# A block with 32 experts on one core: the order of ScalarE's and VectorE's work among the experts, the PSUM banks, and how far weights are split ahead

## The chip, the cores and the metric

The kernel runs on one core of a Trainium2 chip. The metric is the device time of one execution in microseconds. Before the change it is 2903.58 us, the median of three runs (2898.73 to 2910.64).

## The reference, cut to what matters

A first block of two hybrid layers (a linear recurrence beside attention, then a feed-forward network), then a second block with an mLSTM mixer and a mixture of experts, all in float32 for 512 tokens of 1024 channels. The change touches only the experts:

```python
logits = (xt @ w_router + b_router)                  # 512 tokens, 32 experts
top_vals, top_idx = lax.top_k(logits, TOP_K)         # TOP_K = 4
top_gates = jax.nn.softmax(top_vals, axis=-1)
...
def expert_block(args):                              # xb: tokens of one expert
    xb, e = args
    gate = xb @ w_gate[e] + b_gate[e]                # 1024 x 1024
    up = xb @ w_up[e] + b_up[e]                      # 1024 x 1024
    gate = jnp.minimum(gate, SWIGLU_LIMIT)
    up = jnp.clip(up, -SWIGLU_LIMIT, SWIGLU_LIMIT)
    glu = gate * jax.nn.sigmoid(SWIGLU_ALPHA * gate)
    return (glu * (up + 1.0)) @ w_down[e] + b_down[e]
...
y_buf = y_buf * gate_buf[:, None]
out = jax.ops.segment_sum(y_buf, tok_buf, num_segments=T + 1)[:T]
```

Each expert has 12 MB of weights, which are read once: 384 loads of 1 MB.

## The kernel before

**Experts by rank.** `rank` (L1331) sorts the experts by their number of tokens. `ranked` (L1823) runs through them in a fixed order of ranks, `FEW`, that mixes large and small ones. Rank 31 comes first; then, with t for a twin, 1 for one block of 128 tokens and 2 for two blocks: t 2 t t 1 t 2 t t 1 t t 2 t t 1 t t 2 t t 1 t t 2 t t 1 t 1 t. So there are 20 twins, 7 experts of one block (with rank 31) and 5 of two blocks: two of (128, 128) and three of (128, 64).

**A split expert** (one or two blocks) has float32 weights that TensorE multiplies in parts: a tile `w` with the part `hi`, rounded by a ScalarE copy, and the rest `lo`, made by a VectorE subtraction from `raw` (`split`, L244 and L245). A product is then three matmuls (`lin`: x high by hi, x high by lo, x low by hi), or two for a block of 64, whose high and low rows share one operand. **A twin** (`twin`, up to 64 tokens) uses the loaded tile `raw` itself: gate fills one half of TensorE's columns and up the other, and nothing is split.

**Stages of an expert.** gate and up are computed in two halves n = 0, 1 of 512 of the 1024 inner channels (`gate_up`, L1630; `gate_up_twin`, L1657). A half has eight steps, k = 0 to 7, one for each 128 input channels, and each step uses one half-tile of 1024 columns, so a 1 MB load serves two steps. `gated` (L1678) then makes the activations: a Silu on ScalarE (L1693, for twins L1674) and two VectorE operations (L1691 and L1694, for twins L1675 and L1676), four more for a block of 64. `turn` (L1696) transposes them on TensorE and copies them out of PSUM. `down` (L1716) and `down_twin` (L1733) multiply them with eight half-tiles, then the result is scaled on ScalarE (`scaled`, L1766; L1747 for twins) and added into the output by an indirect DMA (`scatter`, L1753). `block` and `find` (L1498, L1512) make the one-hot rows of the next expert's tokens, search their numbers and gate weights with small matmuls and gather their rows; `fetch` (L1536) transposes those rows.

**The loop** interleaves two experts: gate/up half 0 of the current one (with the search for the next one and, after some 4 us, the transposition of the previous one's second activations among its steps), then down of the previous one, then gate/up half 1 of the current one (with the transposition of its first activations at step 0, and after some 4 us the `fetch` of the next one). `tiles` turns a time into a step: 0.9 us a step for a twin, 1.4 for a block of 128, 0.95 more for a block of 64.

**What sets the order.** `with self.tc.manual_schedule(engines={mybir.EngineType.PE})` keeps TensorE's instructions in the order in which the program issues them. The other engines' instructions are put in an order by a planner when the program is built; it goes by its own estimate of when each could start. On the chip each engine then runs its queue in that order, and an instruction that waits holds up those behind it.

**Weights** come out of `weights` (L1607), one half-tile a call:

```python
self.split_ahead(AHEAD + 1)                     # AHEAD = 3
self.catch_up(CU + len(self.later) // CV)       # pending operations, CU = 1, CV = 6
return self.halves.pop(0)
```

`split_ahead` (L1585) issues loads into a ring of nine 1 MB tiles and splits into a ring of four `w`. It goes on until four split halves or twelve halves in all are ready, and the whole halves of twins don't count among the four. `catch_up` (L1612) issues operations of `later`, the list of what follows the last sums: the parts of `gated` and `scaled`.

**PSUM.** The eight banks: four for gate and up (tag `gu`), two for down (`dn`), two for transposes and searches (`tps`). A (128, 128) expert takes four `gu` banks for each half, a twin one.

Of the kernel before, what the change touches and what calls it, by code (L numbers as in the profile page):

```python
# [6 lines left out]
F32 = mybir.dt.float32  # L7
# [10 lines left out]
P = 128  # L18
# [187 lines left out]
class _Kernel:  # L206
# [1124 lines left out]
    def rank(self, tp):  # L1331

        nc, cst, rp, mo = self.nc, self.cst, self.rp, self.mo
        hold = lambda shape, name, dt=F32: rp.tile(shape, dt, name=name)
        keep = lambda shape, name, dt=F32: tp.tile(shape, dt, name=name)
        bank = lambda: self.ps2.tile([P, T], F32, tag="gu", name="gu", bufs=4)
        e32, p32 = cst[:, C_E32:C_E32 + NE], cst[:, C_P32:C_P32 + 1]
        t0 = bank()
        for j in range(4):
            nc.tensor.transpose(t0[0:NE, j * P:(j + 1) * P], self.pos[:, j], self.ident)  # L1340
        pT = mo.tile([P, T], F32R, tag="g", name="pT", bufs=2)[0:NE]
        nc.scalar.activation(pT, t0[0:NE], AF.Copy)
        t1 = bank()
        for j in range(4):
            nc.tensor.transpose(t1[0:96, j * P:(j + 1) * P], self.G[:, j].rearrange("p a e -> p (a e)"), self.ident)
        self.gT = gT = mo.tile([P, T], F32R, tag="g", name="gT", bufs=2)[0:96]
        kc = keep([96, 1], "kc")
        nc.vector.scalar_tensor_tensor(kc, self.cc, 32.0, cst[0:96, C_KEYC:C_KEYC + 1], op0=OP.mult, op1=OP.subtract)
        cmp_ = keep([96, NE], "cmp")
        nc.vector.tensor_scalar(cmp_, self.krow[0:96], kc, None, op0=OP.is_gt)  # L1350
        rk = keep([96, 1], "rk")
        nc.vector.reduce_sum(rk, cmp_, axis=AX.X)
        self.perm = hold([96, NE], "perm", F32R)
        nc.vector.tensor_scalar(self.perm, e32[0:96], rk, None, op0=OP.is_equal)
        pb = keep([NE, NE], "permb", BF16)
        nc.vector.tensor_copy(pb, self.perm[0:NE].bitcast(F32))
        t2 = bank()
        self.mm(t2[0:1, 0:NE], self.p32b[0:NE], pb, True, True)
        self.order = hold([1, NE], "order", I32)
        nc.vector.tensor_copy(self.order, t2[0:1, 0:NE])  # L1360
        self.orderf = hold([1, NE], "orderf")
        nc.vector.tensor_copy(self.orderf, t2[0:1, 0:NE])
        self.split_rows(gT, t1[0:96])
        t3 = bank()
        for j in range(4):
            self.mm(t3[:, NE * j:NE * j + NE], pT[:, j * P:(j + 1) * P], self.perm[0:NE], j == 0, j == 3)
        self.posS = hold([P, 4, NE], "posS")
        nc.vector.tensor_copy(self.posS, t3[:, 0:4 * NE].rearrange("p (j e) -> p j e", j=4))
        self.posB = hold([P, 4, NE], "posB")
        nc.vector.tensor_scalar(self.posB, self.posS, -128.0, None, op0=OP.add)  # L1370
        t4 = bank()
        for j in range(4):
            self.mm(t4[:, NE * j:NE * j + NE], gT[0:64, j * P:(j + 1) * P], self.perm[0:64], j == 0, j == 3)
        self.gates = hold([P, 4, NE, 6], "gates", BF16)
        nc.gpsimd.tensor_copy(self.gates[..., 3:6], self.tok[:, :, None, :].to_broadcast([P, 4, NE, 3]))
        self.parts(self.gates[..., 0:3], t4[:, 0:4 * NE].rearrange("p (j e) -> p j e", j=4),
                   mo.tile([P, 4, NE], F32, tag="bs", name="gr", bufs=4))

        cnt = mo.tile([NE, P], F32R, tag="bs", name="cnt", bufs=4)
        nc.gpsimd.tensor_copy(cnt, self.cc[0:NE].to_broadcast([NE, P]))  # L1380
        t5 = bank()
        self.mm(t5[:, 0:NE], cnt, self.perm[0:NE], True, True)
        self.count = hold([P, NE], "count")
        nc.vector.tensor_copy(self.count, t5[:, 0:NE])

        over = keep([1, NE], "over")
        nc.vector.tensor_tensor(over, self.count[0:1], cst[0:1, C_FEW:C_FEW + NE], op=OP.is_gt)
        most = keep([1, 1], "most")
        nc.vector.reduce_max(most, over, axis=AX.X)
        self.many = hold([1, 1], "many", I32)  # L1390
        nc.vector.tensor_copy(self.many, most)
# [13 lines left out]
    def down_bias(self, j):  # L1405

        nc = self.nc
        y = self.mo.tile([P, D], F32, tag="yy", name="yb", bufs=3)
        for n in range(2):
            p, w = self.ps2.tile([P, T], F32, tag="dn", name="dn", bufs=2), slice(n * T, (n + 1) * T)  # L1410
            self.mm(p, self.gT[:, j * P:(j + 1) * P], self.bd[:, w], True, True)
            nc.scalar.activation(y[:, w], p, AF.Copy)
        nc.gpsimd.dma_start(self.acc_d[j * P:(j + 1) * P, :], y, accum_op=OP.add)
# [170 lines left out]

    def split_ahead(self, n):  # L1585


        nc = self.nc
        while self.todo and len(self.halves) < 2 * NRAW - 6:
            src, i, whole = self.todo[0]  # L1590
            if not whole and sum(lo is not None for _, lo in self.halves) >= n:
                break
            self.todo.pop(0)
            if i == 0:
                self.raw = self.raws[self.nload % NRAW]
                self.nload += 1
                nc.sync.dma_start(self.raw, src)
            raw = self.raw[:, 1024 * i:1024 * i + 1024]
            if whole:
                self.halves.append((raw, None))  # L1600
                continue
            w = self.ws[self.nsplit % (AHEAD + 1)]
            self.nsplit += 1
            self.split(raw, w[:, 0], w[:, 1])
            self.halves.append((w[:, 0], w[:, 1]))

    def weights(self):  # L1607
        self.split_ahead(AHEAD + 1)
        self.catch_up(CU + len(self.later) // CV)
        return self.halves.pop(0)  # L1610

    def catch_up(self, n=None):  # L1612
# [17 lines left out]
    def gate_up(self, n, bsel, blocks, among=()):  # L1630

        nc, mo = self.nc, self.mo
        among = list(among)
        if blocks[0]["twin"]:
            return self.gate_up_twin(n, bsel, blocks[0], among)
        ps = [[self.ps2.tile([P, T], F32, tag="gu", name="gu", bufs=4) for _ in range(2)] for _ in blocks]
        for c in range(4):
            for i in range(2):
                wt = self.weights()
                k = 2 * c + i  # L1640
                for p, b in zip(ps, blocks):
                    for s in range(2):
                        w = slice(s * T, (s + 1) * T)
                        self.product(p[s], b, b["xt"], k, [x if x is None else x[:, w] for x in wt], k == 0, k == KD - 1)
                        if k == 0:
                            o = s * D + n * T
                            self.mm(p[s][0:b["n"]], bsel[:, 0:b["n"]], self.bias[:, o:o + T], False, False)
                self.step(among, k)
        for p, b in zip(ps, blocks):
            b["u%d" % n] = self.slot()[0:b["n"]]  # L1650
            self.later += self.gated(p, b["n"], b["u%d" % n])
# [5 lines left out]
    def gate_up_twin(self, n, bsel, b, among):  # L1657


        p = self.ps2.tile([P, T], F32, tag="gu", name="gu", bufs=4)  # L1660
        for k in range(KD):
            w, _ = self.weights()
            for s in range(2):
# [51 lines left out]

    def down(self, n, blocks):  # L1716
        nc, mo = self.nc, self.mo
        ps = [self.ps2.tile([P, T], F32, tag="dn", name="dn", bufs=2) for _ in blocks]
        for c in range(2):
            for i in range(2):  # L1720
                wt = self.weights()
                for z in range(2):
                    k, w = 2 * i + z, slice(z * T, (z + 1) * T)
                    for p, b in zip(ps, blocks):
                        self.product(p, b, b["h%d" % c], k, [x[:, w] for x in wt], c == 0 and k == 0, c == 1 and k == 3)
        for p, b in zip(ps, blocks):
            if n == 0:
                b["y"] = mo.tile([P, D], F32, tag="yy", name="yy", bufs=3)
            self.later += self.scaled(p, b, n)
        if len(blocks) > 1:  # L1730
            self.catch_up()

    def down_twin(self, b):  # L1733

        nc = self.nc
        p = self.ps2.tile([P, T], F32, tag="dn", name="dn", bufs=2)
        rows = (p[0:64], p[64:P])
        for c in range(2):
            w = [self.weights()[0] for _ in range(4)]
# [83 lines left out]
    def ranked(self, cur, slots, ranks, more=False):  # L1823
# [28 lines left out]
            k = tiles(cur, us)  # L1852
            return [(k + i, f) for i, f in enumerate([f for b in nxt for f in self.fetch(b)])]

        with self.tc.manual_schedule(engines={mybir.EngineType.PE}):
            nxt = start(ranks[0], blocks_of(ranks[0]))
            self.queue(order[1][0])
            self.gate_up(1, *cur, [(0, lambda: self.turn(cur[1], 0))])
# [51 lines left out]

SILU7 = 11.914 / (1.0 + _np.exp(-11.914))
ASIDE = (3, 1)
NRAW = 9
RAW0 = 5
XG = 2
EARLY = 2
CU = 1
# [62 lines left out]
```

## Time and profile before

| | |
|---|---|
| median of three runs | 2903.58 us |
| profiled execution, its span | 2903.9 us, 2902.0 us |
| TensorE (PE) busy | 2728.3 us, 94% |
| VectorE (DVE), ScalarE (ACT) busy | 1583.9 us, 55%; 1124.0 us, 39% |
| mean granted clock of TensorE | 0.972 |
| read from HBM | 607.31 MB |

The first 55% of the span are the first block and the mixer; the experts run from some 1690 us to the last sums at 2875 us. In the views below a line names an engine, a line of the kernel, an operation, and `out<-in` by the program's names. The page's slices are each 1/40 of the span, 72.6 us, and their digits busy shares in tenths. A row of waits gives engine and line, what it waited for, the total in us, how often, and the longest. A row of windows gives a stretch, its length, the busy us of each engine with its instructions, the granted clock of TensorE as a share of 2.4 GHz, the DMA share and GB/s; the sum row adds the stretches of one question. A row of the timeline gives start and length in us, and in brackets the idle time of the engine before it and what ended that. A row of groups gives count, busy us, mean ns, then idle us before them and what ended it.

### The profile page before, as it was taken

What the parts mean: (1) busy time and instruction counts of PE and PEld (TensorE: products, weight loads), DVE (VectorE), ACT (ScalarE), POOL (GpSimd) and SP (SyncE); (2) the same over time, 40 slices, a digit from 0 to 9 for tenths busy, and PEclk for the clock granted to TensorE, in tenths of its full rate; (3) what the DMA queues carried; (4) which work ended last, traced back from release to release, by engine and by line L of the source; (5) the groups of instructions that cost most, each with busy time, mean ns of one, the idle gap of its engine ahead of it and who ended that gap; (6) DMA issues with size and microseconds to landing.
All of it is one profiled execution on the core that took longest, in us unless ns stands there. A gap on an engine that the chain in (4) does not pass through costs nothing. (4 is left out here: it accounts for less than half of the span.)

```text
span 2902.0 us, 33795 instructions
## 1 busy us (share of the span) xinstructions
PE 2728.3 (94%) x12644; PEld 1927.0 (66%) x12644; DVE 1583.9 (55%) x2601; ACT 1124.0 (39%) x1655; POOL 217.6 (7%) x207
## 2 busy tenths in 40 slices
PE   7989999999999999999999889989999999999985
PEld 5677888888877788888777656546446446446452
DVE  7877676365686663333488664354444345335353
ACT  3644442222554442222344344344333334334342
POOL 0100000000000000000011010110100210110100
PEclk8999999999999999999999989999999999999998
DMA  6332446365221233333221586997997998998995
GB/s 230 122 113 93 160 160 223 118 213 165 94 69 59 65 99 102 95 96 99 89 73 62 190 317 266 338 409 295 384 399 304 346 407 354 366 409 320 371 386 214
DMA packets 126078, 629.42 MB, mean 217 GB/s; under 512 B 15632, under 2 KB 19088, under 8 KB 76752
## 3 DMA queue, kind: packets, MB, share of 16 engines
q1 hardware_dynamic: 111744, 593.94, 54.2%
q0 software_dynamic: 8288, 23.86, 3.8%
q10 hardware_dynamic: 5872, 9.36, 0.9%
q8 instruction: 101, 1.65, 0.2%
q14 instruction: 73, 0.60, 0.1%
HBM read 607.31 MB, written 24.38 MB: 218 GB/s over the span
## 5 line engine op out<-in xcount | busy, mean ns | idle before, releaser
L236 PE MATMUL acc<-hh,whi 128*128 128x512 f32 (+1 forms) x1496 | 574.7, 388 | 13.9 <-ACT hh L506 6.2
L236 PE MATMUL acc<-hh,wlo 128*128 128x512 f32 (+1 forms) x1496 | 576.5, 387 | 5.2 <-DVE wlo L245 5.1
L236 PE MATMUL acc<-hl,whi 128*128 128x512 f32 (+1 forms) x1496 | 574.2, 385 | 0.7 <-DVE hl L507 0.7
L245 DVE TENSOR_TENSOR wlo<-raw,whi 128x1024 fp32r<-128x1024 f32 (+2 forms) x253 | 305.6, 1210 | 268.4 <-ACT whi L244 266.7
L245 DVE TENSOR_TENSOR w<-raw,w 128x1024 fp32r<-128x1024 f32 x288 | 341.1, 1219 | 188.7 <-ACT w L244 186.9
L244 ACT ACTIVATE whi<-raw 128x1024 fp32r<-128x1024 f32 (+2 forms) x253 | 258.9, 1024 | 471.5 <-PE acc L236 417.9
L236 PE MATMUL gu<-w,xth 128*128 128x512 f32 x896 | 313.9, 429 | 44.1 <-ACT w L244 29.0
L244 ACT ACTIVATE w<-raw 128x1024 fp32r<-128x1024 f32 x288 | 293.0, 1051 | 111.6 <-PE gu L236 67.5
L236 PEld LDWEIGHTS acc<-hh,whi 128*128 128x128 f32 x1496 | 282.1, 190 | 78.5 <-ACT hh L506 9.0
L236 PEld LDWEIGHTS acc<-hh,wlo 128*128 128x128 f32 x1496 | 283.3, 189 | 62.4 <-DVE wlo L245 6.3
L236 PEld LDWEIGHTS acc<-hl,whi 128*128 128x128 f32 x1496 | 283.6, 190 | 56.4 <-issue 3.1
L236 PE MATMUL gu<-raw,xf 128*64 128x512 f32 x1280 | 305.8, 601 | 0.7 <-ACT xf L1549 0.7
L236 PEld LDWEIGHTS gu<-w,xth 128*128 128x128 f32 x896 | 173.3, 198 | 100.4 <-ACT w L244 42.7
L236 PE MATMUL gu<-w,xtl 128*128 128x512 f32 x448 | 183.4, 409 | 0.0
L236 PEld LDWEIGHTS gu<-raw,xf 128*64 128x64 f32 x1280 | 82.3, 136 | 128.8 <-issue 122.7
L236 PE MATMUL dn<-w,hTh 128*128 128x512 f32 x448 | 148.0, 407 | 20.5 <-ACT w L244 11.5
L236 PE MATMUL dn<-raw,hf 128*64 128x512 f32 x640 | 143.0, 600 | 0.0
L236 PEld LDWEIGHTS dn<-w,hTh 128*128 128x128 f32 x448 | 85.2, 192 | 56.3 <-ACT w L244 17.6
L1675 DVE TENSOR_SCALAR u<-gu 64x512 f32<-64x512 f32 x40 | 27.3, 682 | 159.7 <-ACT g L1674 159.7
L828 DVE TENSOR_TENSOR t<-t,acc 128x512 f32<-128x512 f32 x44 | 30.3, 688 | 143.6 <-PE acc L236 134.6
L236 PEld LDWEIGHTS dn<-raw,hf 128*64 128x64 f32 x640 | 45.3, 138 | 89.8 <-issue 89.7
L1753 POOL DMA_INDIRECT accd<-yy,idx x37 | 58.3, 1576 | 590.8 <-ACT yy L1766 264.3
(685 smaller groups left out, 3914.8 us busy)
## 6 DMA issues: line engine op xcount, KB each, us to landing
raw<-in_wgu SPq DMA_DIRECT2D x256, 1024.0 KB, 12.5
raw<-in_wd SPq DMA_DIRECT2D x128, 1024.0 KB, 12.3
raw<-in_ws SPq DMA_DIRECT2D x220, 512.0 KB, 3.5
adaw<-in_wada SPq DMA_DIRECT2D x72, 512.0 KB, 4.8
raw<-in_wada SPq DMA_DIRECT2D x24, 512.0 KB, 5.0
raw<-in_ws SPq DMA_DIRECT2D x24, 384.0 KB, 3.0
xy<-in_xT SPq DMA_DIRECT2D x16, 256.0 KB, 4.6
raw<-in_ws SPq DMA_DIRECT2D x9, 256.0 KB
```

The costliest lines, as they stand in the source:

```text
L236: self.nc.tensor.matmul(ps, l, r, start=first, stop=last)
L244: self.nc.scalar.activation(hi, src, AF.Copy)
L245: self.nc.vector.tensor_sub(lo, src, hi.bitcast(F32))
L828: nc.vector.tensor_mul(u, s, ps[1])
L1675: lambda: nc.vector.tensor_scalar(u, p[0:64], 8.0, -6.0, op0=OP.min, op1=OP.max),
L1753: self.nc.gpsimd.indirect_dma_start(out=self.acc_d[:, :], out_offset=bass.IndirectOffsetOnAxis(ap=b["idx"][0:m, 0:1], axis=0), in_=b["y"][ ...
```

## The change

ScalarE (Activation) and VectorE (DVE) are kept in program order among the experts, as TensorE is. gate, up and down take their sums from one tag of six banks. `split_ahead` counts whole halves too, so that three halves, of whatever kind, are ahead of the one that is handed out. `weights` issues pending operations first and then the next split.

```diff
-        bank = lambda: self.ps2.tile([P, T], F32, tag="gu", name="gu", bufs=4)
+        bank = lambda: self.ps2.tile([P, T], F32, tag="gu", name="gu", bufs=6)
...
-            p, w = self.ps2.tile([P, T], F32, tag="dn", name="dn", bufs=2), slice(n * T, (n + 1) * T)
+            p, w = self.ps2.tile([P, T], F32, tag="gu", name="dn", bufs=6), slice(n * T, (n + 1) * T)
...
     def split_ahead(self, n):
-        while self.todo and len(self.halves) < 2 * NRAW - 6:
-            src, i, whole = self.todo[0]
-            if not whole and sum(lo is not None for _, lo in self.halves) >= n:
-                break
-            self.todo.pop(0)
+        while self.todo and len(self.halves) < n:
+            src, i, whole = self.todo.pop(0)
...
     def weights(self):
+        self.catch_up(CU + len(self.later) // CV)
         self.split_ahead(AHEAD + 1)
-        self.catch_up(CU + len(self.later) // CV)
         return self.halves.pop(0)
...
-        with self.tc.manual_schedule(engines={mybir.EngineType.PE}):
+        with self.tc.manual_schedule(engines=IN_ORDER):
...
+IN_ORDER = {mybir.EngineType.PE, mybir.EngineType.Activation, mybir.EngineType.DVE}
```

The tags `gu` in `gate_up` and `gate_up_twin` and `dn` in `down` and `down_twin` change in the same way.

## Rows read from the trace of the kernel before

**Rows 1.** The page: mean busy share of the DMA engines in 40 slices.

```profile
DMA  6332446365221233333221586997997998998995
```

**Rows 2.** Waits of PE, 1640 to 2902 us.

```profile
PE gu L236 <- ACT w L244: 29.0, 17, 1.9
PE gu L236 <- DVE w L245: 15.1, 17, 1.1
PE dn L236 <- ACT w L244: 11.5, 7, 1.6
PE dn L236 <- DVE w L245: 7.9, 7, 1.1
PE dn L236 <- DVE yy L1768: 1.1, 3, 0.4
PE dn L236 <- ACT yy L1766: 0.9, 3, 0.3
```

**Rows 3.** Windows of the six places B, the last and the sum.

```profile
2808.00:2828.00 20.00, 17.49 (x77) 9.27 (x76) 9.25 (x10) 9.98 (x13) 1.76 (x1) 0.91 0.89 339
sum 120.00, PE 104.92 PEld 56.24 DVE 56.99 ACT 60.91 POOL 13.39; mean PE 17.49 PEld 9.37 DVE 9.50 ACT 10.15 POOL 2.23
```

**Rows 4.** Windows of the seven places C, two and the sum.

```profile
2105.00:2125.00 20.00, 17.24 (x69) 9.54 (x69) 11.57 (x15) 7.37 (x11) 1.00 (x1) 0.83 1.01 410
2543.00:2563.00 20.00, 17.24 (x73) 9.49 (x73) 11.48 (x15) 8.48 (x12) 1.01 (x1) 0.91 1.01 420
sum 140.00, PE 120.66 PEld 67.38 DVE 85.08 ACT 66.09 POOL 8.98; mean PE 17.24 PEld 9.63 DVE 12.15 ACT 9.44 POOL 1.28
```

**Rows 5.** Windows of places A: sum of six one-block, of five two-block.

```profile
sum 120.00, PE 103.93 PEld 57.71 DVE 72.33 ACT 61.48 POOL 20.19; mean PE 17.32 PEld 9.62 DVE 12.06 ACT 10.25 POOL 3.37
...
sum 100.00, PE 86.19 PEld 44.50 DVE 55.88 ACT 43.21 POOL 7.91; mean PE 17.24 PEld 8.90 DVE 11.18 ACT 8.64 POOL 1.58
```

**Rows 6.** Timeline of ACT at a place B.

```profile
2087.67 0.68 ACT L1747 ACTIVATE yy<-dn,gsl 64x512 f32<-64x512 f32 x1 [7.14 <-PE dn L236]
2088.25 1.99 ACT L244 ACTIVATE w<-raw 128x1024 fp32r<-128x1024 f32 x2
```

**Rows 7.** Timeline of ACT at a place C.

```profile
2113.46 0.59 ACT L1674 ACTIVATE g<-gu 64x512 f32<-64x512 f32 x1 [2.14 <-PE gu L236]
2113.96 3.88 ACT L244 ACTIVATE w<-raw 128x1024 fp32r<-128x1024 f32 x4
```

**Rows 8.** Groups of ACT and PE by line, 1690 to 2876 us.

```profile
L244 ACT ACTIVATE w<-raw 128x1024 fp32r<-128x1024 f32 x283 | 287.8, 1051 | 108.0 <-PE gu L236 67.5 <-PE dn L236 32.2 <-DMA raw<-in_wgu 5.9
...
L236 PE MATMUL gu<-raw,xf 128*64 128x512 f32 x1280 | 305.8, 601 | 0.7 <-ACT xf L1549 0.7
```

**Rows 9.** Timeline of DVE at a place A with one block.

```profile
2060.53 0.69 DVE L245 TENSOR_TENSOR xtl<-tps,xth 128x512 fp32r<-128x512 f32 x1 [11.04 <-ACT xth L244]
2064.05 0.68 DVE L1675 TENSOR_SCALAR u<-gu 64x512 f32<-64x512 f32 x1 [1.23 <-ACT g L1674]
2065.38 4.62 DVE L245 TENSOR_TENSOR w<-raw,w 128x1024 fp32r<-128x1024 f32 x4
```

**Rows 10.** Timeline of PE, end of that twin, and split products at full clock.

```profile
2061.39 1.94 PE L236 MATMUL gu<-raw,xf 128*64 128x512 f32 x8
...
1905.26 0.39 PE L236 MATMUL gu<-w,xtl 128*128 128x512 f32 x1
1905.96 0.39 PE L236 MATMUL gu<-w,xtl 128*128 128x512 f32 x1
```

**Rows 11.** Loads, 1690 to 2876 us; one load of them; PE where it is read.

```profile
DMA packets 62192, 418.99 MB, mean 353 GB/s; under 512 B 8344, under 2 KB 8344, under 8 KB 13839
...
L1597 SPq DMA_DIRECT2D raw<-in_wgu x1: 332/332/332, 2270.2 to 2270.2; - x1
DMA to landing us min/median/max: 14.3/14.3/14.3
...
2282.38 3.65 PE L236 MATMUL gu<-raw,xf 128*64 128x512 f32 x16
```

More of the change, by code (lines that the diff above doesn't have):

```diff
@@ L1635, in gate_up @@
             return self.gate_up_twin(n, bsel, blocks[0], among)
-        ps = [[self.ps2.tile([P, T], F32, tag="gu", name="gu", bufs=4) for _ in range(2)] for _ in blocks]
+        ps = [[self.ps2.tile([P, T], F32, tag="gu", name="gu", bufs=6) for _ in range(2)] for _ in blocks]
         for c in range(4):
@@ L1657, in gate_up_twin @@
     def gate_up_twin(self, n, bsel, b, among):
-        p = self.ps2.tile([P, T], F32, tag="gu", name="gu", bufs=4)
+        p = self.ps2.tile([P, T], F32, tag="gu", name="gu", bufs=6)
         for k in range(KD):
@@ L1717, in down @@
         nc, mo = self.nc, self.mo
-        ps = [self.ps2.tile([P, T], F32, tag="dn", name="dn", bufs=2) for _ in blocks]
+        ps = [self.ps2.tile([P, T], F32, tag="gu", name="dn", bufs=6) for _ in blocks]
         for c in range(2):
@@ L1735, in down_twin @@
         nc = self.nc
-        p = self.ps2.tile([P, T], F32, tag="dn", name="dn", bufs=2)
+        p = self.ps2.tile([P, T], F32, tag="gu", name="dn", bufs=6)
         rows = (p[0:64], p[64:P])
```

## The prediction

> **What bounds the kernel now.** I read the page first, then the waits of TensorE, then the stretches around those waits, then the timeline of ScalarE and VectorE in them, and last the loads. The page shows TensorE busy nearly throughout, and the 16 DMA engines at 0.9 or more in ten of the last seventeen slices, from 1668 us on [rows 1]. Both are averages over stretches with different limits: they say where to look and not what ends last. The change touches only the experts, some 1690 to 2876 us.
>
> There TensorE's waits are nearly all of one kind: it stands before a product with split weights until ScalarE has made the high part and VectorE the low part, 29.0 + 15.1 + 11.5 + 7.9 = 63.5 us in 24 places [rows 2]. The places are three, and in all of them a small ("twin") expert, which needs no split, is followed by one that does. **A**: gate/up half 0 of a split expert after half 1 of a twin (11 places). **B**: gate/up half 1 of a one-block split expert after a twin's down (6). **C**: down of a one-block split expert after a twin's gate/up half 0 (7). The stretches cost the same each time: a B leaves TensorE idle (120 - 104.92) / 6 = 2.51 us [rows 3], a C (140 - 120.66) / 7 = 2.76 us [rows 4], an A (120 - 103.93) / 6 = 2.68 us with one block and (100 - 86.19) / 5 = 2.76 us with two [rows 5].
>
> The weights are not late. ScalarE's splits waited 5.9 us for loads in the whole stretch, and 99.7 us for TensorE; the twins' products, which read the loaded tile itself, waited 0.7 us [rows 8]. What is late is the place of the split in ScalarE's queue. At a B it stood 7.14 us behind the scaling of the twin's output, which needs the end of the twin's down, and only then split [rows 6]; at a C four splits stood behind a Silu that needs the end of the twin's gate/up [rows 7]. TensorE's clock pays too: in each B stretch the granted clock is 0.91, part of the 20 us at 1.2 in place of 2.4 GHz, 0.09 x 20 = 1.8 us lost [rows 3]; of the seven C stretches one shows 0.83 and one 0.91, the others 1.00, together 5.2 us [rows 4].
>
> **The change part by part.**
>
> Program order on ScalarE and VectorE. The call that hands out half j issues the split of half j + 3. While a twin runs its last three halves, the splits of the next three are therefore issued, ahead of the Silu or the scaling that waits for the twin's end.
>
> B: a twin's down hands out its last four halves before its second run of products, half of the 32 x 3.65 / 16 = 7.3 us that it takes [rows 11]. The three high parts (1.05 us each [rows 8]) and low parts (1.15 us each in a run [rows 9]) follow one another in that time, and the scaling comes after them. The fourth split stands behind the scaling (some 0.7 us) and is needed three halves, 4.2 us, after the twin's end. The gap goes: 6 x (2.51 + 1.8) = 25.9 us.
>
> C: the three splits lie in the last three of a twin's eight steps, some 0.9 us each, behind one transposed copy. The third low part may come 2 us after the twin's end, but is needed two halves, 2.8 us, after it. The gap goes: 19.3 + 5.2 = 24.5 us.
>
> A, one block: here the order brings its own wait. At the third half TensorE transposes the twin's second activations, which need two VectorE operations on the twin's sums. In the trace they run from 2064.05, ahead of the low parts at 2065.38 [rows 9]. In program order the first stands behind four low parts and the second behind five, the next block's one-hot rows (0.69 us as the copies of that size) and three small ones. From the first copy at 2060.53: two copies 1.4, five low parts at 4.62 for four some 5.7, one-hot 0.7, small ones 0.6, the two operations 1.4, and 0.3 until the first high part: 10.1 us, so 2070.6. TensorE's twin ends at 2063.2 [rows 10]; then three halves at 1.40 us (0.70 for three products), two bias products 0.47 and the search 0.2: 2068.1. It waits some 2.4 us instead of 2.68: 6 x 0.3 = 1.8 us won. Between both ends: none of the gap goes (0), or all of it (16.1).
>
> A, two blocks: the same queue has one or two copies more, some 10.8 to 11.5 us, but the halves before that transposition last 5.8 to 6.7 us, so that 0.7 to 1.4 us are left. I take 1.1 of 2.76: 5 x 1.7 = 8.5 us. The clock lost there may come back (some 1.8 us each as at a B, 9) or not (0); a wait stays, so I take 0.
>
> New: a (128, 64) expert's second activations go through four more operations, handed out while the following twin's halves run, at 0.9 us each instead of 1.4. The twin comes to their transposition at its fifth half. No row shows this wait. It is at best nothing and at most the 2.76 of rows 4; near the wait of A with two blocks I take 1.2: 3 x 1.2 = 3.6 us lost. It can't gain, since nothing waits there now.
>
> Banks. gate, up and down rotate through six banks, where gate/up had four and down two. TensorE stood 0.9 + 1.1 = 2.0 us before a down whose bank was not yet read [rows 2]; that may go. At worst a two-block expert, which takes four banks per half, waits for one copy (0.7 us) in each of ten halves: 7 us. I take 0, nearest to the row.
>
> Four halves made ahead, whole ones counted. A load is now issued in the program at most two tiles ahead, where before twins let it run six ahead. SyncE's queue holds only loads and register reads, each load waits for its slot of nine and not for the program around it, so the order on SP stays and the cost is nothing; had SP to wait for more, it would be priced as the loads below. POOL's order is left free; its gather gets its indices up to 3 us later, behind the low parts of A, and its rows are turned a down (7.3 us or more) after that, which covers it.
>
> Swapping the two lines in the hand-out puts the pending operation ahead of the split; on the path only in A, where it is counted.
>
> What is late next: the loads. Everything won lies in stretches where the DMA share is 1.01 and 410 to 420 GB/s move [rows 4]; only the last B has a share of 0.89 [rows 3]. Near the end of two twins in a row there is no reserve: the load issued at 2270.2 landed 14.3 us later, at 2284.5, and the product that reads it, the fifth step of the twin, began at some 2285.0 (2282.38 plus three steps of four products at 3.65 / 16) [rows 11]. Three times the order runs two twins, one block, two twins, two blocks; there, what A, B and C win before the second pair is waited for at its end: 3 x (4.3 + 3.5 + 0.3 + 1.7) = 29.4 us given back. The other cycles have one twin in place of the second pair and keep their gain. Bounds: nothing given back, or all.
>
> Sum: 25.9 + 24.5 + 1.8 + 8.5 - 3.6 = 57.1; less 29.4 = 27.7 us. The profiled execution took 2903.9 us (span 2902.0), within 0.4 us of the median of 2903.58, so the sum stands against either: 2876 us.
>
> **The rivals.**
>
> *Loads give back everything.* The C shown lie under a full DMA share; if no buffer covers them, all is given back and the time stays some 2899 us (the last B alone is kept, some 4.3 us). For: rows 4 and 11. Against: seven of the last seventeen slices stand at 0.5 to 0.8 [rows 1]; in them the ring of nine fills again.
> The Trainium skill ("DMA: Bandwidth & Descriptors", Where 436 GB/s comes from) says that for transfers from HBM the core's share of HBM binds, at some 358 GB/s. By that rule the 418.99 MB of this stretch need 1170 of its 1186 us [rows 11], and at most 16 us could be won. The trace disagrees: it shows 410 to 420 GB/s for 20 us at a time [rows 4], at which 418.99 MB need some 1020 us.
>
> *Loads give back little.* The nine slots refill while the large experts run; then 57 us are won, with A's clock 66: 2838 to 2847 us.
>
> *Slower: VectorE in order becomes the bound.* Eight low parts take 9.1 us of a one-block phase of 11.7 us, and three to five operations of 0.7 us come on top. If every one of the 36 phases of split experts waited as the A above, 36 x 2.4 = 86 us, less 57: 2933 us. It decides from 57 / 36 = 1.6 us a phase. For: the queue worked out at A. Against: in B and C nothing that waits for TensorE stands before the low parts.
>
> *The order was already that of the program.* Excluded by rows 6 and 7: the program has the split before the scaling.
>
> **How the numbers follow.** Forecast (part given back) 0.50, little given back 0.20, everything given back 0.20, slower 0.10. What a measurement can tell from no change is 0.5%, 14.5 us: 2889 and 2918. The forecast and the second lie below 2889 nearly whole, the third and fourth hardly: faster 0.72, same 0.19, slower 0.09. The range goes from 2848 (little given back, some clock not) to 2898 (nearly everything given back); it leaves out some 0.07 below and 0.13 above. The forecast's own range is 2862 to 2889.
>
> **What would show it.** Right: the waits for w of 63.5 us fall below 15; at a B ScalarE splits before it scales; a wait of the transposition of activations for VectorE appears, some 15 places of 1 to 2.5 us; products that read raw tiles wait for loads. Wrong: if B's gap stays, the order isn't what I read; if waits for loads exceed 50 us, the third case; if low parts are late in halves far from a twin, the fourth.

## The result, and the profile after

The changed kernel takes 2858.48 us (median of four runs, 2857.36 to 2862.15) against 2903.97 us beside it: a ratio of 0.9844, 95% interval 0.9822 to 0.9867. That is 45.5 us less, where 27.7 were predicted. The profiled execution took 2859.26 us (span 2857.3, mean granted clock 0.978 after 0.972).

The whole gain lies among the experts. A window from the first product of their gate/up to the end of the last down, first of the kernel before, then of the one after (us, TensorE's busy us, the other engines', granted clock, DMA share, GB/s):

```profile
1690.19:2875.14 1184.95, 1112.22 (x5081) 622.83 (x5079) 520.59 (x656) 450.10 (x606) 123.91 (x103) 0.97 0.90 354
```

```profile
1690.10:2830.02 1139.92, 1091.75 (x5073) 612.48 (x5071) 522.99 (x656) 450.39 (x606) 118.23 (x102) 0.98 0.93 367
```

The stretch is 45.0 us shorter: TensorE's idle time falls from 72.7 to 48.2 us, and its busy time by 20.5 us with nearly the same instructions. That is mostly the clock: added up over windows of 20 us, this stretch loses some 40 us of full-speed time to it before and some 23 after. TensorE's waits from 1640 us on, after (what it waited for, us, times, longest):

```profile
PE tps L1700 <- DVE u L1672: 19.0, 12, 2.4
PE dn L236 <- DMA raw<-in_wd: 8.9, 6, 2.7
PE tps L236 <- DVE oh L1503: 6.5, 5, 3.8
...
PE gu L236 <- ACT w L244: 4.2, 3, 1.7
...
PE gu L236 <- DVE w L245: 2.8, 5, 0.8
PE tps L1700 <- DVE u L1690: 2.8, 3, 0.9
```

Against [rows 2], the waits for split weights fell from 63.5 to 7.0 us, and those of down are gone. In their place stand the second activations of a twin (u, line 1672; 3.0 us before), loads (raw), and the four operations of a (128, 64) expert (line 1690): three times 0.9 us, where 1.2 were priced. The places B and C, in the manner of [rows 3, 4], one stretch of B, then the sums of its six and of the seven of C:

```profile
2060.00:2080.00 20.00, 20.00 (x96) 12.06 (x95) 12.21 (x12) 11.09 (x13) 2.35 (x2) 1.00 1.01 400
...
sum 120.00, PE 120.00 PEld 72.31 DVE 73.01 ACT 67.05 POOL 13.30; mean PE 20.00 PEld 12.05 DVE 12.17 ACT 11.18 POOL 2.22
...
sum 140.00, PE 140.00 PEld 82.69 DVE 94.54 ACT 72.27 POOL 8.13; mean PE 20.00 PEld 11.81 DVE 13.51 ACT 10.32 POOL 1.16
```

TensorE is busy all of the time there, and in all thirteen the granted clock is 1.00. ScalarE's timeline at the first B shows why (start, length, operation, idle time before it):

```profile
1887.10 2.00 ACT L244 ACTIVATE w<-raw 128x1024 fp32r<-128x1024 f32 x2 [3.36 <-DMA raw<-in_wgu]
1889.53 1.06 ACT L244 ACTIVATE w<-raw 128x1024 fp32r<-128x1024 f32 x1 [0.43 <-DMA raw<-in_wgu]
1890.88 0.69 ACT L1743 ACTIVATE yy<-dn,gsl 64x512 f32<-64x512 f32 x1 [0.29 <-PE dn L236]
```

Three splits now stand ahead of the scaling, where [rows 6] had the scaling first after 7.14 us of idling. But the releaser is new: the splits wait for loads. So it is in the whole group, 37.3 us where [rows 8] had 5.9 (ScalarE's splits, us busy, mean ns, idle before them by releaser):

```profile
L244 ACT ACTIVATE w<-raw 128x1024 fp32r<-128x1024 f32 x282 | 289.9, 1052 | 90.4 <-DMA raw<-in_wgu 37.3 <-PE gu L236 30.5 <-PE dn L236 17.8
```

At A little idle time is won. The two sums as in [rows 5], first the six stretches with one block, then the five with two:

```profile
sum 120.00, PE 99.98 PEld 51.01 DVE 67.82 ACT 62.75 POOL 22.82; mean PE 16.66 PEld 8.50 DVE 11.30 ACT 10.46 POOL 3.80
...
sum 100.00, PE 91.08 PEld 47.10 DVE 54.30 ACT 45.28 POOL 16.37; mean PE 18.22 PEld 9.42 DVE 10.86 ACT 9.06 POOL 3.27
```

TensorE is idle for 20.0 + 8.9 = 28.9 us there, before for 16.1 + 13.8 = 29.9. At an A with one block, VectorE's queue has the order worked out at [rows 9]:

```profile
1871.39 0.69 DVE L1503 TENSOR_TENSOR oh<-cst,posS 128x512 bf16<-128x512 f32 x1
1872.00 1.22 DVE L245 TENSOR_TENSOR w<-raw,w 128x1024 fp32r<-128x1024 f32 x1
1873.13 0.68 DVE L1671 TENSOR_SCALAR u<-gu 64x512 f32<-64x512 f32 x1
1873.73 1.21 DVE L245 TENSOR_TENSOR w<-raw,w 128x1024 fp32r<-128x1024 f32 x1
...
1875.43 0.68 DVE L1672 SCALAR_TENSOR_TENSOR u<-g,u 64x512 f32<-64x512 f32 x1
```

The first operation on u stands behind low parts and a one-hot row, the second behind one low part more. What was not worked out stands ahead of them, in ScalarE's queue: the first split of this expert waits for its load, and TensorE's first product waits 1.69 us for that split.

```profile
1866.30 1.06 ACT L244 ACTIVATE w<-raw 128x1024 fp32r<-128x1024 f32 x1 [3.42 <-DMA raw<-in_wgu]
```

Yet the clock was won at A. Two of the eleven stretches before, one with one block and one with two, and the two after that answer to them (the last three columns are clock, DMA share, GB/s):

```profile
2055.00:2075.00 20.00, 17.19 (x79) 8.84 (x76) 10.46 (x14) 10.05 (x14) 2.97 (x3) 0.91 1.02 412
2156.00:2176.00 20.00, 17.27 (x72) 8.53 (x69) 10.03 (x15) 8.13 (x12) 1.75 (x2) 0.83 1.02 410
```

```profile
2037.00:2057.00 20.00, 16.63 (x83) 8.69 (x80) 11.68 (x15) 10.96 (x15) 4.21 (x3) 1.00 1.02 412
2134.00:2154.00 20.00, 17.11 (x79) 9.19 (x79) 9.82 (x14) 8.45 (x13) 2.62 (x3) 0.91 1.02 411
```

Over all eleven, one minus the granted clock sums to 0.94 before and 0.41 after; times 20 us that is 18.8 and 8.2 us of full-speed time lost. Two of the windows after end just as the clock falls (at 2278.7 and at 2698.6 us); with these slow stretches counted whole, the places lose 10.2 us after. And the clock falls where it did not before: in two of the downs that wait for loads, from 2121.7 and from 2555.2 us on, 3.4 us lost each. A part of the first of either kind:

```profile
2279.00:2282.00 3.00, 3.00 (x8) 2.32 (x8) 1.48 (x2) 1.64 (x2) 0.64 (x1) 0.50 1.02 431
2122.00:2128.00 6.00, 4.92 (x12) 1.45 (x14) 0.00 (x0) 0.00 (x0) 0.00 (x0) 0.50 1.02 427
```

Both stand at 1.2 GHz.

### The profile page after: what moved, and what is told of

Same layout as the page of the kernel before. It is cut to its first block, busy times and chain, and to the rows that moved or that the text cites. A ratio compares the mean times of both kernels' runs of the same rounds, so it can differ in the third digit from the quotient of the medians.

```text
span 2857.3 us, 33816 instructions
## 1 busy us (share of the span) xinstructions
PE 2707.6 (95%) x12644; PEld 1917.2 (67%) x12644; DVE 1586.8 (56%) x2601; ACT 1125.2 (39%) x1655; POOL 213.3 (7%) x207
## 5 line engine op out<-in xcount | busy, mean ns | idle before, releaser
L236 PE MATMUL gu<-w,xth 128*128 128x512 f32 x896 | 302.5, 419 | 8.0 <-ACT w L244 4.2
L236 PE MATMUL dn<-raw,hf 128*64 128x512 f32 x640 | 152.8, 619 | 8.9 <-DMA raw<-in_wd 8.9
L236 PE MATMUL dn<-w,hTh 128*128 128x512 f32 x448 | 140.8, 395 | 0.0
L236 PEld LDWEIGHTS gu<-w,xtl 128*128 128x128 f32 x448 | 86.3, 193 | 20.1
```

The costliest lines, as they stand in the source:

```text
L236: self.nc.tensor.matmul(ps, l, r, start=first, stop=last)
```

## Experiments

Runs on different chips are compared by their ratio to the kernel before on the same chip.

**Which engine's order.** Three runs of the changed kernel, with fewer engines in program order (the sets are shortened here).

```diff
-        with self.tc.manual_schedule(engines=IN_ORDER):
+        with self.tc.manual_schedule(engines={mybir.EngineType.PE}):          # no_order
+        with self.tc.manual_schedule(engines={..PE, ..Activation}):           # act_only
+        with self.tc.manual_schedule(engines={..PE, ..DVE}):                  # dve_only
```

> The changed kernel with program order on TensorE alone: shared banks, four halves ahead and the swapped lines stay. Theory (the gain is the place of the splits in ScalarE's queue): nearly all of it goes, 2890 to 2912 us, and the waits of TensorE for the split weights in the experts come back at 50 to 70 us. Rival (banks and the shorter look-ahead bring a good part themselves): 2880 us or less, with those waits under 45 us.

> The changed kernel with TensorE and ScalarE in program order, VectorE's order left free. Theory (ScalarE's queue holds the high parts back, and a low part can only follow its high part): most of the gain stays, 2855 to 2872 us, and no place waits 2 us for ScalarE. Rival (VectorE's own order holds the low parts back; TensorE waited 23.0 us for low parts before): 2880 us or more, with 20 us or more of waits for low parts.

> The changed kernel with TensorE and VectorE in program order, ScalarE's order left free. Theory: ScalarE still scales or does its Silu before it splits, so nothing is won, and VectorE in order now stands behind the late high parts: 2895 to 2930 us. Rival (VectorE's order was the culprit): 2880 us or less.

Measured: TensorE alone 2898.87 us, ratio 0.9995 (0.9984 to 1.0006); with ScalarE 2858.87 us, 0.9858 (0.9840 to 0.9875); with VectorE 2916.69 us, 1.0058 (1.0045 to 1.0071). In the first the waits for split weights are back, 30.7 + 14.9 + 11.5 + 7.9 = 65.0 us in the same 24 places. TensorE's largest waits in the second and the third:

```profile
PE dn L236 <- DMA raw<-in_wd: 10.4, 8, 2.6
PE tps L1700 <- DVE u L1672: 8.3, 7, 2.2
PE gu L236 <- DVE w L245: 6.7, 10, 0.8
PE gu L236 <- ACT w L244: 6.0, 4, 2.1
```

```profile
PE gu L236 <- ACT w L244: 27.2, 15, 2.1
PE tps L1700 <- DVE u L1672: 22.1, 12, 2.4
PE dn L236 <- ACT w L244: 11.5, 7, 1.6
```

All three came as the theory had them, save one ScalarE wait of 2.1 us in the second, where none of 2 was expected. Of the three orders, ScalarE's brings the whole gain, with the other edits in place. VectorE's order on top of it changes nothing that the times can tell (0.9858 and 0.9844, with overlapping intervals). Without ScalarE's it costs: the waits for ScalarE's high parts stay, and the 22.1 us of waits for u come on top, although 23.0 us of the waits before were put down to VectorE. With ScalarE alone in order, that share falls to some 7: the low part was only the last link of a late high part.

**Are look-ahead and line order free?** The kernel before with the order and the banks alone, and then the changed kernel with each of the two others put back. (The order without the shared banks was not tried.)

```diff
 order_banks, against the kernel before: engines and the tags of six banks as in the change, nothing else
 ahead_back, against the changed kernel:
-        while self.todo and len(self.halves) < n:
-            src, i, whole = self.todo.pop(0)
+        while self.todo and len(self.halves) < 2 * NRAW - 6:
+            src, i, whole = self.todo[0]
+            if not whole and sum(lo is not None for _, lo in self.halves) >= n:
+                break
+            self.todo.pop(0)
 swap_back, against the changed kernel, in weights():
-        self.catch_up(CU + len(self.later) // CV)
         self.split_ahead(AHEAD + 1)
+        self.catch_up(CU + len(self.later) // CV)
```

> The kernel before with program order on the three engines and the shared banks; its own look-ahead (up to twelve halves, four of them split) and the order of the two lines in the hand-out stay. Theory (both of these count for nothing, as predicted): within 6 us of the changed kernel's 2858.5, so 2853 to 2865 us. Rival (in order, a split handed out a whole twin ahead makes ScalarE stand before a load that has not landed, and what is queued behind it waits): 2870 us or more, with ScalarE's idle time before splits caused by loads well above the 38.8 us of the changed kernel.

> The changed kernel with the look-ahead of before alone put back (twins' halves not counted, up to twelve); the swapped lines stay. Theory (from the run before: a split handed out a whole twin ahead waits for its load, and ScalarE in order keeps the twin's activations behind it): 2905 to 2925 us, with 50 to 70 us of TensorE's waits for the copies of turned activations (hf). Rival (the order of the two lines in the hand-out did it): 2850 to 2868 us, no such waits.

> The changed kernel with the two lines of the hand-out in the order of before (split first, pending operation second). Theory: 2852 to 2870 us, since a split now handed out three halves ahead has its tile; waits of the second activations (u) for VectorE grow by at most one low part, 1.15 us, in 11 places. Rival (the lines did it): 2900 us or more.

Measured: order and banks alone 2916.02 us, 1.0055 (1.0041 to 1.0068): my theory fell, the rival held. The old look-ahead alone 2914.68 us, 1.0055 (1.0039 to 1.0072); the old lines alone 2867.21 us, 0.9898 (0.9881 to 0.9914). In the first of them TensorE's largest wait, a transposition by TensorE and ScalarE's timeline at one such place, and ScalarE's splits as a group:

```profile
PE tps L1540 <- ACT hf L1707: 61.5, 8, 8.8
```

```profile
2054.14 0.46 PE L1704 MATMUL tps<-cst,u 64*128 64x64 f32 x4
...
2060.42 2.00 ACT L244 ACTIVATE w<-raw 128x1024 fp32r<-128x1024 f32 x2 [13.43 <-DMA raw<-in_wgu]
...
2064.88 1.39 ACT L1747 ACTIVATE yy<-dn,gsl 64x512 f32<-64x512 f32 x2
2066.30 0.38 ACT L1707 ACTIVATE hf<-tps 128x256 f32<-128x256 f32 x1
```

```profile
L244 ACT ACTIVATE w<-raw 128x1024 fp32r<-128x1024 f32 x283 | 294.2, 1056 | 294.9 <-DMA raw<-in_wgu 128.7 <-PE gu L236 94.6 <-PE dn L236 37.8
```

Four splits, handed out a whole twin ahead, waited 13.43 us for a load. The copy of the twin's activations behind them in the queue (2066.30) waited with them, its bank stayed taken, and TensorE's next transposition stood still, eight times for up to 8.8 us. The look-ahead alone brings this back (54.4 us in 8 places). So "four halves, whole ones counted" is what makes ScalarE's order pay: without it the order loses 0.55%. The swapped lines are worth some 0.5%, about 15 us; with the old ones the waits for u grow from 19.0 to 27.3 us, 0.7 us a place, and where the rest lies is not shown. Both came as expected. The Trainium skill ("PSUM — Partial Sum Buffer", Engine vs sequencer instructions) calls the queues of ScalarE and VectorE strict FIFO; the trace agrees for ScalarE, where the copy, whose transposition had ended at 2054.6, runs only at 2066.30, behind the splits.

**What the loads cost.** Half of each twin's bytes are not loaded, in the changed kernel and in the one before.

```diff
-                nc.sync.dma_start(self.raw, src)
-            raw = self.raw[:, 1024 * i:1024 * i + 1024]
+                if whole:
+                    nc.sync.dma_start(self.raw[:, 0:1024], src[:, 0:1024])
+                else:
+                    nc.sync.dma_start(self.raw, src)
+            raw = self.raw[:, 0:1024] if whole else self.raw[:, 1024 * i:1024 * i + 1024]
```

> The changed kernel with half of each twin's bytes not loaded: a twin's odd halves read the tile's first half again, so 20 x 6.3 MB of 419 MB fall away; all instructions stay. Theory (what loads take back is what is missing to the 57.1 us of the sum, 57.1 - 45.5 = 12 us): 2840 to 2850 us, waits of products and splits for loads under 1 us. Rival (loads take nothing back, the terms of order were over-counted): 2855 us or more. Second rival (loads take back the 29.4 us that I priced): 2832 us or less.

> The kernel before with the same half of each twin's bytes not loaded. Theory (before, loads held nothing up: 5.9 us of ScalarE's waits and 0.7 us of the twins'): 2895 to 2905 us, no change within 0.5%. Rival (part of what the changed kernel won is load time that the kernel before lost too): 2888 us or less.

Measured: 2818.45 us, 0.9726 (0.9710 to 0.9742), and 2799.34 us, 0.9659 (0.9643 to 0.9676). Both theories fell; the second rival of the first and the rival of the second held by their times. The changed kernel's loop with short loads, and its sums at A with one block and with two:

```profile
1690.00:2787.75 1097.75, 1072.32 (x5065) 607.48 (x5063) 518.69 (x654) 447.10 (x604) 115.84 (x100) 0.99 0.76 266
```

```profile
sum 120.00, PE 107.48 PEld 60.20 DVE 75.57 ACT 65.79 POOL 24.46; mean PE 17.91 PEld 10.03 DVE 12.60 ACT 10.97 POOL 4.08
...
sum 100.00, PE 96.05 PEld 52.04 DVE 57.80 ACT 50.19 POOL 17.06; mean PE 19.21 PEld 10.41 DVE 11.56 ACT 10.04 POOL 3.41
```

In the changed kernel the left-out half of the twins' bytes costs 1139.92 - 1097.75 = 42.2 us, more than the second rival's 29.4: 22.7 us idle and 19.4 us of busy time. At A the idle time is 12.5 + 4.0 = 16.5 us, 2.1 us a place with one block (2.4 worked out) and 0.8 with two (1.1): the order does there what was predicted, and the loads took it. TensorE's waits say the same: those for split weights (7.0 us), for a low part of the activations (xtl, 2.9) and 3.2 of the 6.5 us for one-hot rows (oh) are gone in the light run.

The kernel before is no clean test of loads. Its loop, and ScalarE at the first B, where the twin's down runs from 1877.85 us on:

```profile
1690.22:2770.02 1079.80, 1067.79 (x5069) 603.76 (x5067) 521.95 (x654) 457.12 (x604) 114.25 (x100) 1.00 0.77 271
```

```profile
1875.23 1.06 ACT L244 ACTIVATE w<-raw 128x1024 fp32r<-128x1024 f32 x1 [0.36 <-PE gu L236]
1877.27 0.60 ACT L1696 ACTIVATE g<-gu 128x512 f32<-128x512 f32 x1 [0.97 <-PE gu L236]
1877.77 1.99 ACT L244 ACTIVATE w<-raw 128x1024 fp32r<-128x1024 f32 x2
1885.01 1.40 ACT L1750 ACTIVATE yy<-dn,gsl 64x512 f32<-64x512 f32 x2 [5.25 <-PE dn L236]
```

The planner, which orders ScalarE by its own estimate of when a tile is there, now put the splits (1877.77) ahead of the scaling itself. Only the bytes differ, so the old order came from its estimate of the loads, and [rows 8] show that the real ones were there (5.9 us of waits). What order alone, with the old sequence and short loads, would give stays open: shorter loads change the sequence. The run does show how short the loop can get when loads and order fit: 1079.80 us with 12.0 us idle at a clock of 1.00, 18.0 less than program order with the same bytes, which waits 18.7 us for u where the planner's order waits 2.2.

**Winning the rest.** The waits at A are taken away by handing out the transposition later (turn7); the same experts are put in another order (smooth); both; and then one of four buffers of split halves is made a tenth slot for loads (slot_traded).

```diff
 turn7
-                among = [(tiles(cur[1], 4), lambda: self.turn(prev[1], 1))]
+                among = [(tiles(cur[1], 4 if cur[1][0]["twin"] else 7), lambda: self.turn(prev[1], 1))]
 smooth, the sequence of ranks (11 to 30 are twins)
-       [11, 0, 12, 13, 5, 14, 2, 15, 16, 6, 17, 18, 1, 19, 20, 7, 21, 22, 3, 23, 24, 8, 25, 26, 4, 27, 28, 9, 29, 10, 30])
+       [11, 12, 5, 13, 0, 14, 15, 6, 16, 2, 17, 18, 7, 19, 1, 20, 21, 8, 22, 23, 3, 24, 25, 9, 26, 4, 27, 28, 10, 29, 30])
 slot_traded, with both edits above
-NRAW = 9
+NRAW = 10
-AHEAD = 3
+AHEAD = 2
```

> The changed kernel with the transposition of the twin's second activations handed out later in the split expert that follows (sixth half in place of the third with one block, third in place of the second with two). Theory: the 19.0 us of waits for u fall below 4 us, but the loads, which limit the pairs of twins, take back about half: 2842 to 2854 us. Rival (what is won at A is not under a load limit): 2840 us or less. Second rival (the later transposition makes down wait for it): 2862 us or more.

> The changed kernel with another order of the same experts: the twenty twins stand as 3, 3, 3, 4, 3, 4 between the large experts, with a one-block expert among them each time, in place of 1, 3, 4, 4, 4, 4. Bytes and instructions are the same. Theory (the loads fall behind only where four twins and one one-block expert follow one another, and the nine slots cover three): at least half of the 42 us between the changed kernel and its light version comes back, 2820 to 2838 us, and waits of products for loads fall below 3 us. Rival (all 419 MB at the rate that the loads reach set the loop's time, whatever the order): 2852 to 2864 us.

> Both edits at once. Theory: with the loads relieved by the order, the later transposition wins most of its 18 us (the difference of the two light loops): 2806 to 2826 us. Rival (loads take it back as before): within 5 us of the run with the order alone.

> The run with both edits (2845.8 us), with one of the four buffers of split halves turned into a tenth slot for loads, so three halves are made ahead in place of four. Theory (loads are the limit now; a tenth slot lets the loads run one tile, some 2.5 us at 410 GB/s, further ahead through each of the six stretches of twins): 2828 to 2842 us, waits of TensorE for loads fall below 4 us. Rival (two halves of lead are too few for the splits in order: the first product after a twin waits again): 2850 us or more, with waits for split weights above 20 us.

Measured: later transposition 2852.85 us, 0.9838 (0.9820 to 0.9856); other sequence 2850.91 us, 0.9826 (0.9809 to 0.9842); both 2845.84 us, 0.9804 (0.9786 to 0.9821); with the tenth slot 2831.89 us, 0.9762 (0.9742 to 0.9781).

The first edit did to the waits what its theory said, and its gain went to the loads, nearly all of it and not half; the time lies in the theory's range only because the kernel before is faster on this chip (2857 us by the ratio). Its waits, and ScalarE's splits:

```profile
PE dn L236 <- DMA raw<-in_wd: 13.3, 10, 2.7
...
PE tps L1700 <- DVE u L1672: 2.2, 1, 2.2
```

```profile
L244 ACT ACTIVATE w<-raw 128x1024 fp32r<-128x1024 f32 x281 | 289.7, 1053 | 117.3 <-DMA raw<-in_wgu 59.0 <-PE gu L236 31.0 <-PE dn L236 17.0
```

16.8 us of waits for u are gone; products wait 4.4 us more for loads and splits 21.7 us more, and by the ratios it can't be told from the changed kernel. The sequence fell short of its theory: 6.6 us of waits of products for loads stay, and by its ratio it ends among the times of its rival (2853 us). Both together missed as well, within 5.1 us of the sequence alone. The tenth slot brought the time that the theory said, 0.4% below the run with both edits and 0.8% below the changed kernel, and its interval meets neither of theirs. The waits of products for loads in down did not fall below 4 us, they rose from 7.3 to 9.7; what fell, from 63.2 to 29.2 us, is what ScalarE's splits wait for loads (with both edits, then with the tenth slot):

```profile
L244 ACT ACTIVATE w<-raw 128x1024 fp32r<-128x1024 f32 x284 | 292.9, 1053 | 121.9 <-DMA raw<-in_wgu 63.2 <-PE gu L236 31.3 <-PE dn L236 17.8
...
L244 ACT ACTIVATE w<-raw 128x1024 fp32r<-128x1024 f32 x280 | 291.4, 1054 | 115.1 <-PE gu L236 57.8 <-DMA raw<-in_wgu 29.2 <-PE dn L236 23.6
```

Its loop, and TensorE's waits:

```profile
1690.18:2804.28 1114.10, 1080.97 (x5058) 601.73 (x5056) 522.79 (x653) 454.61 (x604) 129.85 (x100) 1.00 0.96 376
```

```profile
PE dn L236 <- DMA raw<-in_wd: 9.7, 8, 2.2
PE gu L236 <- DVE w L245: 9.2, 16, 0.8
...
PE gu L236 <- ACT w L244: 3.3, 3, 1.9
```

The DMA share is 0.96, the granted clock 1.00, and two halves of lead are enough: 12.5 us of waits for split weights, not the 20 of the rival. It is the fastest kernel here that does the whole work. The slot without the other two edits was not tried.

## Why the prediction came out 17.5 us too high

What the prediction named as signs of being right came: waits for split weights of 7.0 us, splits ahead of the scaling at a B, 15 waits of a transposition for VectorE (19.0 + 2.8 us), and products of raw tiles that wait for loads.

**B and C.** Right to the term: 25.9 and 24.5 us were priced, and thirteen stretches without idle time at a clock of 1.00 give just that.

**A, the idle time.** 1.8 + 8.5 = 10.3 us were priced. The order gives 29.9 - 16.5 = 13.4 with short loads, but only 0.9 with real ones.

**A, the clock: the step that failed.** The prediction said "a wait stays, so I take 0". The upper bound of 9 us was for five stretches, and I had looked at the clock of B and C only. All eleven lost 18.8 us before and 10.2 after, so 8.6 came back although waits stayed: of two stretches about as idle (2055 before, 2037 after, above) one shows 0.91, the other 1.00. Before, the waits stood at the first products; after, the largest stands at the third half. That this makes the difference was not tried by itself, and it does not hold throughout: after waits of 2.37 to 2.39 us at the third half the clock fell at 2278.7 and 2698.6 us and stayed at 2054 and 2488. The cause is open.

**The new wait.** 3.6 us priced, 2.8 measured.

**The loads.** 29.4 us were priced. B, C, A's clock, and A as short loads leave it, less the new wait, make 25.9 + 24.5 + 8.6 + 13.4 - 2.8 = 69.6 us; 45.0 were won, so 24.6 us were given back. The trace shows where: 12.5 us of idle time at A, 8.9 of waits for loads in down, and 6.8 of clock in two of those downs, together 28.2; why that is 3.6 more than the sum leaves stays open. I had placed all of it in three cycles, at their second pair of twins. The waits in down lie there and nowhere else, and so do 5.0 of the 12.5 us, at the A behind them; the other 7.5 lie at one-block experts, where I had priced nothing, and I had no term for the clock of a late down. So the place was right in part, and that the size came near is partly luck.

The 42.2 us that the light run won are 17.6 more than these 24.6. Idle time outside the 24 places is not the reason (8.4 us before, 9.0 in the light run). Most of it is busy time of TensorE, 39.9 us less in the light run than before, of which the clock makes some 30; where the rest comes from stays open.

**Edits priced at nothing.** Without the order, banks, look-ahead and the swapped lines together win nothing (0.9995). With it, no wait for a bank is left where 2.0 us were before (the banks alone were not tried), and the swapped lines bring some 0.5%. "Nothing" hid what the look-ahead is for: I asked what it does to SyncE's queue and not to ScalarE's, where it decides the sign.

**The rivals.** Loads giving back everything fell: 45 us were won. So did the rule of the Trainium skill ("DMA: Bandwidth & Descriptors", Where 436 GB/s comes from) named beside it, that some 358 GB/s bind transfers from HBM: the loop moved 367 GB/s, and 376 with the tenth slot. Loads giving back little fell as a mechanism, though its 2838 to 2847 us end nearer to the time than the forecast. VectorE as the bound fell: its order is worth nothing either way once ScalarE's is right.

## What to carry to other kernels

When an engine is put in program order, read for each instruction that the program hands out early what it waits for, and what stands behind it in that queue: a look-ahead that is harmless to a planner stops the whole engine when its load is late. Price the clock at every place that a change touches, also where a wait stays. And ask what a late load costs beside its wait: here it also lowered the clock in two downs. Once the waits on engines were gone and the loop's DMA share stood at 0.93, it was a buffer for loads, taken from a lead that did not need it, that brought more (0.4%), while later transpositions and another sequence brought hardly anything.

## What was not expected of the hardware

Of the 45.0 us, 20.5 came as shorter busy time of TensorE with nearly the same instructions, the mean granted clock of the loop going from 0.97 to 0.98; with the tenth slot it is 1.00 although loads still hold down up 8 times, by at most 2.2 us. And TensorE can lose much to a late load that its rows of waits put down to others: between the changed kernel and its light version lie 42.2 us, of which rows that name a DMA make 9.1. Another 13.5 are put down to ScalarE and VectorE, whose work stands behind a split that waits for its load, and of the 19.4 us of busy time the clock makes some 12.
